# An FFN unit's first product is copied by ScalarE into the PSUM bank on which TensorE adds the second

## The chip, the core and the metric

The kernel runs on one core of a Trainium2 chip. The metric is the device time of one execution in microseconds (us). Before the change it is 1089.62 us, the median of three runs (1089.29 to 1091.97). Five engines work side by side, each through its own queue in order: TensorE (PE; its weight loads are PEld), VectorE (DVE), ScalarE (ACT), GpSimd (POOL) and SyncE (SP, which issues the loads). They wait for each other by semaphores.

## The reference

One layer of a backbone for 512 noisy tokens and 128 context tokens, 1024 features each: a gated recurrence, a spatial gating MLP and a pooling mixer, merged by gates, then a ConvFFN. The change touches the ConvFFN alone:

```python
def conv_ffn(x, w_up, conv_w, conv_b, w_down):
    h = x @ w_up                                  # 1024 -> 2 * 2816
    hp = jnp.pad(h, ((0, 0), (1, 1), (0, 0)))
    h = hp[:, :-2] * conv_w[0] + hp[:, 1:-1] * conv_w[1] + hp[:, 2:] * conv_w[2] + conv_b
    a, b = jnp.split(h, 2, axis=-1)
    return (jax.nn.silu(a) * b) @ w_down
```

## The kernel before

Everything is float32. TensorE takes operands of a reduced type, so each is split into a high and a low part, and a product of 128 features is three matmuls (`mm3`, L194 to L196: high·high, high·low, low·high). ScalarE writes the high part (`high`, L1159), VectorE the low one (`low`, L1164).

The FFN's up-projection goes by units `p` of 128 features of `a` and the 128 features of `b` that multiply them: 22 units (`NFF`). Unit 0 is computed plainly. Units 1 to 21 multiply 2x2 blocks (two halves of the 1024 input features, two halves of 320 tokens) with seven products in place of eight. A product is 4 blocks of 128 features, 12 matmuls of 320 columns, which TensorE adds up in a PSUM bank. In the order in which TensorE makes them in a unit, and with the name of the operand by which a row of the trace tells them:

1. m1 = `A10` on `b11`, into bank a
2. m2 = `A11` on `b21`, into bank b
3. n5 = `s` on `q1`, into bank c
4. `t` on `q2`, added to bank a
5. `A22` on `q4`, added to bank a of the unit before (`last`)
6. `u` on `b22`, added to bank c
7. `w` on `t3`, added to bank a

Between them the banks are read out, since later products are added to the same bank. `evacuate(p, 0, ...)` (ScalarE, L1212) copies m1 out of bank a into `ev`, before `t` is added there; `evacuate(p, 1, ...)` copies n5 out of bank c before `u`; `evacuate(p, 2, ...)` copies bank a after `t`, before `w`. The first half of `a`'s features, `u[:, 0, 0:H]` = m1 + m2, is an add on VectorE (L1222, 128x320), which reads bank b and `ev`. The other three quarters are two adds on VectorE and one copy on ScalarE (L1423).

The convolution of a finished unit follows one unit later: `conv_first` (ScalarE, L1233) makes the middle tap and the bias, `conv_rest` (VectorE, L1239, two instructions) the outer taps, then SiLU (ScalarE, L1391) and the product with the other half (`ffn_gate`, VectorE, L1245). The weight blocks' sums for the next unit are VectorE's: `sums` (L1143, L1144) and `sums2` (L1149, L1150). What is split for the next unit: `A1` = raw weights, `s` = sum, `tu` = sums, `wA` = raw sums; nine buffers (`WBUFS`) hold the parts.

The order on TensorE, ScalarE, VectorE and GpSimd is the order in which the code issues the instructions (`manual_schedule`); no planner is at work in this stage. Each waits at its place until the semaphores that it needs are there, and all behind it on its engine wait with it. From unit 3 on (`EARLY`) m1 and m2 of a unit are issued in its own turn of the loop; m1 and m2 of units 1 and 2 are made ahead of the loop. `u` has two buffers, `ev` two, PSUM eight banks.

After the 22 units TensorE makes the down-projection (L194 to L196 on `ah`).

Of the kernel before, what the change touches and what calls it, by code (L numbers as in the profile page):

```python
# [9 lines left out]
F32 = mybir.dt.float32  # L10
F32R = mybir.dt.float32r
I32 = mybir.dt.int32
AF = mybir.ActivationFunctionType
# [3 lines left out]
P = 128  # L17
# [8 lines left out]
H = HALF  # L26
# [37 lines left out]
def block_kernel(ctx: ExitStack, tc, x_prompt, x_sample, state, w_ada, w_in, w_bhg, w_bsg,  # L64
# [3 lines left out]
    nc = tc.nc  # L68
    ctx.enter_context(tc.manual_schedule(engines={mybir.EngineType.PE}))

    def pool(stack, name, bufs=1, space=None, side="left"):
        kw = {"side": side}
        if space is not None:
            kw = {"space": space}
        return stack.enter_context(tc.tile_pool(name=name, bufs=bufs, reuse_waits="tile", **kw))
# [33 lines left out]
    def par(name, i=0, n=1):  # L109
        a = PK[name][0] + i  # L110
        return pk[:, a:a + n]
# [34 lines left out]
    def half_of(t, n):  # L146
        return t[:, n * HK:(n + 1) * HK, :]
# [43 lines left out]
    def mm3(out, ws, xs, first, last, more=False):  # L191

        (wh, wl), (xh, xl) = ws, xs
        nc.tensor.matmul(out, lhsT=wh, rhs=xh, start=first, stop=False, skip_group_check=more)  # L194
        nc.tensor.matmul(out, lhsT=wh, rhs=xl, start=False, stop=False, skip_group_check=more)  # L195
        nc.tensor.matmul(out, lhsT=wl, rhs=xh, start=False, stop=last, skip_group_check=more)  # L196
# [619 lines left out]
    hz = pool(hzst, "hz", side="right")  # L816
# [218 lines left out]
    def quarter(pl, name):  # L1035
        return tuple(pl.tile([P, HK, H], F32R, tag="bf", name=name + part, bufs=6) for part in "hl")

    b11, b21, b22 = (quarter(bp, name) for name in ("b11", "b21", "b22"))
# [84 lines left out]
    def up_tile():  # L1123
        return ps_f.tile([P, 512], F32, tag="up", name="up")[:]
# [9 lines left out]
    raws, forms, banks, us, evs, accs = {}, {}, {}, {}, {}, {}  # L1134

    def up_raw(p, s):
        return wraw(unit_parts(cols_unit(ffn_up, (p + s * NFF) * P)), KD)
# [14 lines left out]
    def high(p, what, src, room=None):  # L1152

        room = room or wpair(src)
        if len(src.shape) == 3 and src.shape[1] == HK:
            hi, lo = room[0][:, 0:HK, :], room[0][:, HK:KD, :]
        else:
            hi, lo = room
        nc.scalar.activation(hi, src, AF.Copy)  # L1159
        forms[p, what] = (hi, lo, src)  # L1160

    def low(p, what):
        hi, lo, src = forms[p, what]
        nc.vector.tensor_tensor(lo, src, hi.bitcast(F32), op=ALU.subtract)  # L1164

    def one_form():
        return (wpool.tile([P, 1024], F32R, tag="w", name="ws", bufs=WBUFS)[:].rearrange("p (k c) -> p k c", k=KD),)

    def of(p, what, n=None):
        hi, lo = forms[p, what][0:2]  # L1170
        return (hi, lo) if n is None else (half_of(hi, n), half_of(lo, n))
# [18 lines left out]
    def product(p, what, bank, xs, first=False):  # L1190
        if what[0:2] == "A1":
            hi, lo = forms[p, "A1"][0:2]
            n = int(what[2])
            ws = (half_of(hi, n), lo[n] if isinstance(lo, list) else half_of(lo, n))
        elif what == "s":
            ws = of(p, "s")
        else:
            ws = of(p, *{"t": ("tu", 0), "u": ("tu", 1), "w": ("wA", 0), "A22": ("wA", 1)}[what])
        for k in range(HK):
            mm3(bank[:, 0:H], tuple(w[:, k, :] for w in ws), tuple(x[:, k, :] for x in xs),  # L1200
                first and k == 0, k == HK - 1, not first)

    def early(p, n):
        if n == 0:
            banks[p, "a"] = up_tile()
            product(p, "A10", banks[p, "a"], b11, True)
        else:
            banks[p, "b"] = up_tile()
            product(p, "A11", banks[p, "b"], b21, True)

    def evacuate(p, n, bank):
        nc.scalar.activation(evs[p][:, n, :], bank[:, 0:H], AF.Copy)  # L1212

    def pieces(u, half):

        if half == 0:
            return [(u[:, 0:H], slice(0, H))]
        return [(u[:, H:TS], slice(0, TS - H)), (u[:, TS + GAP:TF], slice(TS - H, H))]

    def add_to(u, half, bank, ev):  # L1220
        for to, c in pieces(u, half):
            nc.vector.tensor_tensor(to, bank[:, c], ev[:, c], op=ALU.add)  # L1222

    def conv_weight(p, s, r):

        return nconv[:, 3 * p + r:3 * p + r + 1] if s and p else par("conv_w", 3 * (p + s * NFF) + r)

    def conv_first(p, s, tag):

        jj = p + s * NFF  # L1230
        w = conv_weight(p, s, 1)
        accs[p, s] = hz.tile([P, TF], F32, tag=tag, name="acc", bufs=2)
        nc.scalar.activation(accs[p, s][:], us[p][:, s, :], AF.Identity, bias=par("conv_b", jj), scale=w)  # L1233

    def conv_rest(p, s):
        w0, w2 = (conv_weight(p, s, r) for r in (0, 2))
        acc, u = accs[p, s], us[p][:, s, :]
        for w, o, x in ((w0, acc[:, 1:TF], u[:, 0:TF - 1]), (w2, acc[:, 0:TF - 1], u[:, 1:TF])):
            nc.vector.scalar_tensor_tensor(o, x, w, o, op0=ALU.mult, op1=ALU.add)  # L1239

    def clear_gap(p, s):
        nc.gpsimd.memset(us[p][:, s, TS:TS + GAP], 0.0)
# [30 lines left out]
    EARLY = 3  # L1273
# [77 lines left out]
    for p in range(1, NFF + 1):  # L1351
        real, last, nxt = p < NFF, p - 1, p + 1 < NFF
        summed = last > 0
        if nxt:
            for s in range(2):
                if (p + 1, s) not in raws:
                    raws[p + 1, s] = up_raw(p + 1, s)

        if real and p >= EARLY:
            early(p, 0)  # L1360
        conv_first(last, 0, "gz")
        if summed:
            add_to(us[last][:, 1, :], 1, banks[last, "a"], evs[last][:, 1, :])
            clear_gap(last, 1)
        if real:
            low(p, "wA")

        if real:
            if p >= EARLY:
                early(p, 1)  # L1370
            evs[p] = hz.tile([P, 4, H], F32, tag="xk", name="ev", bufs=2)
            evacuate(p, 0, banks[p, "a"])
        conv_rest(last, 0)

        if real:
            banks[p, "c"] = up_tile()
            product(p, "s", banks[p, "c"], q1, True)
            if nxt and p + 1 >= EARLY:
                high(p + 1, "A1", raws[p + 1, 0])
            us[p] = hz.tile([P, 2, TF], F32, tag="tot", name="u", bufs=2)  # L1380
            add_to(us[p][:, 0, :], 0, banks[p, "b"], evs[p][:, 0, :])
            if nxt:
                sums(p + 1)

            product(p, "t", banks[p, "a"], q2)
            evacuate(p, 1, banks[p, "c"])
            if not summed:
                evacuate(p, 2, banks[p, "a"])
            if nxt:
                high(p + 1, "s", forms[p + 1, "sum"], one_form())  # L1390
        nc.scalar.activation(accs[last, 0][:], accs[last, 0][:], AF.Silu)  # L1391
        if nxt:
            if p + 1 >= EARLY:
                low(p + 1, "A1")
            low(p + 1, "s")

        if not real:
            pss = [[(slice(0, 512), up_tile())] for i in range(NT)]
            ws = unit(rows_unit(ffn_down, 0, 0), 0)
            for k in range(2):  # L1400
                for i in range(NT):
                    down(i, 0, k, ws)
        if summed:
            product(last, "A22", banks[last, "a"], q4)
        if real and summed:
            evacuate(p, 2, banks[p, "a"])
        if nxt:
            sums2(p + 1)
        elif real:
            fetch(1)  # L1410
            parts.update({(0, k): act_parts(k) for k in range(2)})
        else:
            fetch(1)
            parts.update({(0, k): act_parts(k) for k in range(2, 4)})

        if real:
            product(p, "u", banks[p, "c"], b22)
        if summed:
            ffn_gate(last - 1)
        if nxt:  # L1420
            high(p + 1, "tu", raws[p + 1, 0])
        if summed:
            nc.scalar.activation(us[last][:, 1, 0:H], banks[last, "a"][:, 0:H], AF.Copy)  # L1423
        if nxt:
            low(p + 1, "tu")

        if real:
            product(p, "w", banks[p, "a"], t3)
        conv_first(last, 1, "sig")
        if nxt:  # L1430
            high(p + 1, "wA", raws[p + 1, 1])
        if real:
            add_to(us[p][:, 0, :], 1, banks[p, "c"], evs[p][:, 2, :])
            clear_gap(p, 0)
        conv_rest(last, 1)
# [156 lines left out]
```

## Time and profile before

| | |
|---|---|
| median of three runs | 1089.62 us |
| the profiled execution, its own time | 1089.21 us |
| its span in the trace | 1087.4 us |
| outside the span | 1.8 us |
| units 1 to 21 of the FFN | about 666 to 935 us of the span |
| down-projection | about 926 to 1080 us |
| TensorE busy | 1059.7 us (97%) |
| VectorE busy | 761.2 us (70%) |
| ScalarE busy | 505.5 us (46%) |

A matmul's record is longer than the distance to the next one, since matmuls overlap in the array: rows of TensorE are read by the distance of their starts. The same holds in a smaller measure on VectorE and ScalarE, where the next instruction starts some hundredths of a microsecond before the record of the one ahead ends. A number in brackets behind a row is the idle time ahead of it and the engine that ended it. In the windows, PEclk is the clock that TensorE was granted, as a share of its full speed.

### The profile page before, as it was taken

Reading aid. Unit: us, or ns where it says so; the run is one execution under the profiler, and the core shown is the slowest. Engines: PE = TensorE matmul, PEld = TensorE weight load, DVE = VectorE, ACT = ScalarE, POOL = GpSimd, SP = SyncE. Lnnn points to the kernel's source line nnn. Section 1 sums busy time; section 2 is a strip of 40 time slices with the busy share of each in tenths; the row PEclk is TensorE's granted clock in tenths of the full one; section 3 lists DMA queues with packets and bytes.
Section 4 is the critical chain, followed back from the end, with each engine's and each line's share of the span. In section 5 each row is a group of like instructions: output and inputs, shape, how many; then the busy total and the mean of one; then the engine's idle time right before and its main releaser. Section 6 shows DMA issues by size and latency. Waiting matters only on the chain.

```text
span 1087.4 us, 17828 instructions
## 1 busy us (share of the span) xinstructions
PE 1059.7 (97%) x7258; PEld 989.7 (91%) x7258; DVE 761.2 (70%) x1141; ACT 505.5 (46%) x846; POOL 43.2 (4%) x111
## 2 busy tenths in 40 slices
PE   6999999999999999999999998999999999999997
PEld 4789999988999999999998888999999999888886
DVE  5586845677454767768365588999999998854634
ACT  5565533244324344533332356555555555643432
POOL 1030000000000000000000110000000000000201
PEclk9999999999999999999999999999999999999999
DMA  9964556535373121211135321322223222622202
GB/s 291 334 220 127 184 157 183 189 105 182 93 233 125 48 68 47 62 30 40 44 99 193 117 78 59 91 85 79 78 78 91 85 87 89 252 97 78 78 1 97
DMA packets 151618, 126.98 MB, mean 117 GB/s; under 512 B 4688, under 2 KB 131936, under 8 KB 151024
## 3 DMA queue, kind: packets, MB, share of 16 engines
q1 hardware_dynamic: 150816, 124.53, 36.9%
q8 instruction: 57, 0.93, 0.4%
q10 hardware_dynamic: 720, 1.31, 0.3%
q14 instruction: 25, 0.20, 0.1%
HBM read 115.32 MB, written 10.50 MB: 116 GB/s over the span
## 4 chain that ended last, share of the span: by engine, by line
PE 67%; DVE 24%; ACT 4%; issue 4%; DMA 2%; SPq 0%; POOL 0%; POOLq 0%; DVEq 0%; ACTq 0%
DVE wl L1164 7%; PE up L196 6%; PE up L195 6%; PE mm L195 6%; PE mm L194 6%; PE mm L196 6%; PE up L194 6%; DVE acc L1239 5%; PE q L194 4%; PE q L195 4%; PE q L196 4%; PE scores L891 4%; DVE u L1222 3%; ACT wh L1159 2%; PE px L194 2%
## 5 line engine op out<-in xcount | busy, mean ns | idle before, releaser
L125 DVE TENSOR_TENSOR wl<-raw,wh 128x1024 fp32r<-128x1024 f32 (+1 forms) x105 | 123.7, 1182 | 91.3 <-ACT wh L124 35.9
L124 ACT ACTIVATE wh<-raw 128x1024 fp32r<-128x1024 f32 (+1 forms) x105 | 107.2, 1022 | 63.1 <-PE q L195 28.6
L194 PE MATMUL mm<-h1h,wh 128*128 128x320 f32 x384 | 122.8, 320 | 0.0
L196 PE MATMUL mm<-h1h,wl 128*128 128x320 f32 x384 | 118.6, 309 | 0.0
L195 PE MATMUL mm<-h1l,wh 128*128 128x320 f32 x384 | 118.6, 309 | 0.0
L195 PE MATMUL up<-wl,ah 128*128 128x512 f32 (+1 forms) x242 | 89.9, 372 | 0.2 <-DVE wl L125 0.2
L196 PE MATMUL up<-wh,ah 128*128 128x512 f32 (+1 forms) x242 | 89.6, 370 | 0.1
L194 PE MATMUL up<-wh,ah 128*128 128x512 f32 (+1 forms) x242 | 89.7, 371 | 0.0
L1159 ACT ACTIVATE wh<-raw 128x1024 fp32r<-128x1024 f32 x63 | 66.2, 1051 | 43.1 <-DVE raw L1150 43.1
L1164 DVE TENSOR_TENSOR wl<-raw,wh 128x1024 fp32r<-128x1024 f32 x63 | 76.9, 1220 | 9.7 <-ACT wh L1159 9.6
L195 PEld LDWEIGHTS mm<-h1l,wh 128*128 128x128 f32 x384 | 72.3, 188 | 0.0
L194 PEld LDWEIGHTS mm<-h1h,wh 128*128 128x128 f32 x384 | 72.3, 188 | 0.0
L196 PEld LDWEIGHTS mm<-h1h,wl 128*128 128x128 f32 x384 | 72.1, 188 | 0.0
L124 ACT ACTIVATE ah<-act 128x512 fp32r<-128x512 f32 x88 | 36.2, 462 | 64.4 <-PE up L196 62.6
L125 DVE TENSOR_TENSOR ah<-act,ah 128x512 fp32r<-128x512 f32 x88 | 38.8, 486 | 33.0 <-ACT ah L124 33.0
L194 PE MATMUL q<-h1h,wh 128*128 128x320 f32 x192 | 60.0, 313 | 0.0
L196 PE MATMUL q<-h1h,wl 128*128 128x320 f32 x192 | 59.3, 309 | 0.0
L195 PE MATMUL q<-h1l,wh 128*128 128x320 f32 x192 | 59.3, 309 | 0.0
L195 PEld LDWEIGHTS up<-wl,ah 128*128 128x128 f32 x242 | 45.6, 188 | 8.7 <-DVE wl L125 0.9
L196 PEld LDWEIGHTS up<-wh,ah 128*128 128x128 f32 x242 | 45.6, 188 | 8.2 <-DVE ah L125 0.4
L194 PEld LDWEIGHTS up<-wh,ah 128*128 128x128 f32 x242 | 45.6, 188 | 7.9
L1159 ACT ACTIVATE ws<-s 128x512 fp32r<-128x512 f32 x21 | 13.3, 633 | 60.6 <-DVE s L1143 60.6
(373 smaller groups left out, 2996.0 us busy)
## 6 DMA issues: line engine op xcount, KB each, us to landing
raw<-in_w_in SPq DMA_DIRECT2D x56, 512.0 KB
raw<-in_ffn_up SPq DMA_DIRECT2D x44, 512.0 KB
raw<-in_w_ada SPq DMA_DIRECT2D x32, 512.0 KB
raw<-in_ffn_down SPq DMA_DIRECT2D x22, 512.0 KB
raw<-in_w_ada SPq DMA_DIRECT2D x32, 256.0 KB
raw<-in_w_out SPq DMA_DIRECT2D x8, 512.0 KB
x2scr<-x SPq DMA_DIRECT2D x5, 512.0 KB
x<-x2scr SPq DMA_DIRECT2D x1, 2560.0 KB
```

Source lines behind the costliest of these rows:

```text
L124: nc.scalar.activation(hi, src, AF.Copy)
L125: nc.vector.tensor_tensor(lo, src, hi.bitcast(F32), op=ALU.subtract)
L194: nc.tensor.matmul(out, lhsT=wh, rhs=xh, start=first, stop=False, skip_group_check=more)
L195: nc.tensor.matmul(out, lhsT=wh, rhs=xl, start=False, stop=False, skip_group_check=more)
L196: nc.tensor.matmul(out, lhsT=wl, rhs=xh, start=False, stop=last, skip_group_check=more)
L891: nc.tensor.matmul(px[:, i, :], lhsT=ck[:, i * P:(i + 1) * P], rhs=rhs(i), start=True, stop=True)
L1159: nc.scalar.activation(hi, src, AF.Copy)
L1164: nc.vector.tensor_tensor(lo, src, hi.bitcast(F32), op=ALU.subtract)
L1222: nc.vector.tensor_tensor(to, bank[:, c], ev[:, c], op=ALU.add)
L1239: nc.vector.scalar_tensor_tensor(o, x, w, o, op0=ALU.mult, op1=ALU.add)
```

## The change

For units 3 to 21 (`seeded`), ScalarE copies m1 from bank a into bank b, at the head of its work for the unit, and TensorE adds m2 there (`product` without `first`). n5 moves between m1 and m2 on TensorE. Bank b then holds m1 + m2; ScalarE copies it to `u[:, 0, 0:H]`, after n5's copy, and VectorE's add is gone. For units 1 and 2 the add stays, and m1's copy moves ahead of `conv_first`.

```diff
-        if real and p >= EARLY:
+        seeded = real and p >= EARLY
+        if seeded:
             early(p, 0)
+            banks[p, "b"] = up_tile()
+            nc.scalar.activation(banks[p, "b"][:, 0:H], banks[p, "a"][:, 0:H], AF.Copy)
+        elif real:
+            evs[p] = hz.tile([P, 4, H], F32, tag="xk", name="ev", bufs=2)
+            evacuate(p, 0, banks[p, "a"])
         conv_first(last, 0, "gz")
         if summed:
             add_to(us[last][:, 1, :], 1, banks[last, "a"], evs[last][:, 1, :])
             clear_gap(last, 1)
         if real:
             low(p, "wA")
-
-        if real:
-            if p >= EARLY:
-                early(p, 1)
-            evs[p] = hz.tile([P, 4, H], F32, tag="xk", name="ev", bufs=2)
-            evacuate(p, 0, banks[p, "a"])
         conv_rest(last, 0)
...
             us[p] = hz.tile([P, 2, TF], F32, tag="tot", name="u", bufs=2)
-            add_to(us[p][:, 0, :], 0, banks[p, "b"], evs[p][:, 0, :])
+            if seeded:
+                evs[p] = hz.tile([P, 4, H], F32, tag="xk", name="ev", bufs=2)
+
+                product(p, "A11", banks[p, "b"], b21)
+            else:
+                add_to(us[p][:, 0, :], 0, banks[p, "b"], evs[p][:, 0, :])
             if nxt:
                 sums(p + 1)

             product(p, "t", banks[p, "a"], q2)
             evacuate(p, 1, banks[p, "c"])
+            if seeded:
+                nc.scalar.activation(us[p][:, 0, 0:H], banks[p, "b"][:, 0:H], AF.Copy)
```

ScalarE, one unit in the middle of the FFN, before: from the copy of the unit before last to SiLU. `up_7481` is this unit's bank a, `up_7517` its bank c; L1212 is a copy into `ev`, L1233 `conv_first`, L1159 a high part.

```order
L1423 ACTIVATE u_7265<-up_7213 128x320
L1233 ACTIVATE acc_7467<-u_7265,pk_96,nconv_5886 128x644
L1159 ACTIVATE wh_7469<-raw_7345 128x1024
L1233 ACTIVATE acc_7494<-u_7399,pk_96 128x644
L1212 ACTIVATE ev_7513<-up_7481 128x320
L1159 ACTIVATE wh_7530<-raw_7477 128x1024
L1212 ACTIVATE ev_7513<-up_7517 128x320
L1159 ACTIVATE ws_7551<-s_7535 128x512
L1391 ACTIVATE acc_7494<-acc_7494 128x644
```

The same stretch on ScalarE in the changed kernel, where `up_7481` is bank a, `up_7494` bank b and `up_7504` bank c.

```order
L1430 ACTIVATE u_7252<-up_7213 128x320
L1233 ACTIVATE acc_7467<-u_7252,pk_96,nconv_5886 128x644
L1159 ACTIVATE wh_7469<-raw_7345 128x1024
L1363 ACTIVATE up_7494<-up_7481 128x320
L1233 ACTIVATE acc_7496<-u_7386,pk_96 128x644
L1159 ACTIVATE wh_7517<-raw_7477 128x1024
L1212 ACTIVATE ev_7521<-up_7504 128x320
L1393 ACTIVATE u_7520<-up_7494 128x320
L1159 ACTIVATE ws_7551<-s_7534 128x512
L1398 ACTIVATE acc_7496<-acc_7496 128x644
```

The copy of bank a (L1212 before, L1363 now) has moved ahead of `conv_first`, writes a bank instead of `ev`, and a copy of bank b (L1393) has come in ahead of `ws`.

TensorE, another unit, before: the end of m1 (`b11`) and what follows it.

```order
L194 MATMUL up_7347<-b11h_5877,wh_7262 128x320
L195 MATMUL up_7347<-b11l_5878,wh_7262 128x320
L196 MATMUL up_7347<-b11h_5877,wl_7263 128x320
L194 MATMUL up_7366<-b21h_5879,wh_7262 128x320
L195 MATMUL up_7366<-b21l_5880,wh_7262 128x320
L196 MATMUL up_7366<-b21h_5879,wl_7263 128x320
```

The same unit on TensorE in the changed kernel, at the start of m2 (`b21`).

```order
L194 MATMUL up_7370<-q1h_6384,ws_7283 128x320
L195 MATMUL up_7370<-q1l_6385,ws_7283 128x320
L196 MATMUL up_7370<-q1h_6384,ws_7283 128x320
L194 MATMUL up_7360<-b21h_5879,wh_7249 128x320
L195 MATMUL up_7360<-b21l_5880,wh_7249 128x320
L196 MATMUL up_7360<-b21h_5879,wl_7250 128x320
```

m2 stood right behind m1, and now stands behind n5 (`q1`), one product later.

## Rows read from the trace of the kernel before

**Rows 1.** The page: busy time of each engine, its share of the span, and its instructions.

```profile
PE 1059.7 (97%) x7258; PEld 989.7 (91%) x7258; DVE 761.2 (70%) x1141; ACT 505.5 (46%) x846; POOL 43.2 (4%) x111
```

**Rows 2.** The chain of waits in the stretch from 706 to 909 us: share of the stretch by engine and line.

```profile
by line: DVE wl L1164 28.2%; DVE acc L1239 20.0%; issue 11.9%; DVE u L1222 11.1%; ACT wh L1159 8.4%; DVE raw L1150 5.5%; DVE raw L1149 4.8%; DVE s L1143 4.8%; DVE ws L1164 4.7%; DVE raw L1144 0.3%; DVEq L1144 0.2%; ACTq L1159 0.1%
```

**Rows 3.** The windows, 693.1 to 909 us: length, busy us (and instructions) of PE, PEld, DVE, ACT and POOL, granted clock, DMA share, GB/s.

```profile
693.10:909.00 215.90, 213.85 (x1431) 209.54 (x1430) 205.92 (x307) 123.25 (x187) 2.25 (x34) 1.00 0.29 84
```

**Rows 4.** The timeline of VectorE over one unit: start us, us, engine, line, operation, out<-in.

```profile
756.74 0.48 DVE L1222 TENSOR_TENSOR u<-up,ev 128x320 f32<-128x320 f32 x1
757.14 0.68 DVE L1143 TENSOR_TENSOR s<-raw 128x512 f32<-128x512 f32 x1
...
760.92 0.69 DVE L1150 TENSOR_TENSOR raw<-raw 128x512 f32<-128x512 f32 x1
...
762.80 1.23 DVE L1164 TENSOR_TENSOR wl<-raw,wh 128x1024 fp32r<-128x1024 f32 x1 [0.45 <-ACT wh L1159]
...
767.73 1.81 DVE L1239 SCALAR_TENSOR_TENSOR acc<-u,pk,acc 128x643 f32<-128x643 f32 x2
769.45 0.48 DVE L1222 TENSOR_TENSOR u<-up,ev 128x320 f32<-128x320 f32 x1
769.85 0.69 DVE L1143 TENSOR_TENSOR s<-raw 128x512 f32<-128x512 f32 x1
```

**Rows 5.** The timeline of ScalarE over the same unit.

```profile
757.86 0.64 ACT L1159 ACTIVATE ws<-s 128x512 fp32r<-128x512 f32 x1 [3.11 <-DVE s L1143]
758.40 0.73 ACT L1391 ACTIVATE acc<-acc 128x644 f32<-128x644 f32 x1
759.03 0.41 ACT L1212 ACTIVATE ev<-up 128x320 f32<-128x320 f32 x1
761.71 1.06 ACT L1159 ACTIVATE wh<-raw 128x1024 fp32r<-128x1024 f32 x1 [2.27 <-DVE raw L1150]
762.68 0.42 ACT L1423 ACTIVATE u<-up 128x320 f32<-128x320 f32 x1
...
764.02 1.04 ACT L1159 ACTIVATE wh<-raw 128x1024 fp32r<-128x1024 f32 x1
764.97 0.91 ACT L1233 ACTIVATE acc<-u,pk 128x644 f32<-128x644 f32 x1
765.79 0.41 ACT L1212 ACTIVATE ev<-up 128x320 f32<-128x320 f32 x1
766.10 1.05 ACT L1159 ACTIVATE wh<-raw 128x1024 fp32r<-128x1024 f32 x1
767.05 0.42 ACT L1212 ACTIVATE ev<-up 128x320 f32<-128x320 f32 x1
770.57 0.63 ACT L1159 ACTIVATE ws<-s 128x512 fp32r<-128x512 f32 x1 [3.10 <-DVE s L1143]
```

**Rows 6.** The timeline of TensorE over the same unit: the end of `u`, the start of `w`, then the first matmul of m1, m2, n5 and `t`.

```profile
759.05 0.31 PE L196 MATMUL up<-b22h,wl 128*128 128x320 f32 x1
759.50 0.41 PE L194 MATMUL up<-t3h,wh 128*128 128x320 f32 x1
759.75 0.31 PE L195 MATMUL up<-t3l,wh 128*128 128x320 f32 x1
...
761.36 0.31 PE L194 MATMUL up<-b11h,wh 128*128 128x320 f32 x1
...
763.12 0.31 PE L194 MATMUL up<-b21h,wh 128*128 128x320 f32 x1
...
764.88 0.31 PE L194 MATMUL up<-q1h,ws 128*128 128x320 f32 x1
...
766.64 0.31 PE L194 MATMUL up<-q2h,wh 128*128 128x320 f32 x1
```

**Rows 7.** Two groups of ScalarE's instructions from 690 to 909 us (count, busy us, mean ns of one, idle us before them), and one short instruction from its timeline.

```profile
L1159 ACT ACTIVATE wh<-raw 128x1024 fp32r<-128x1024 f32 x52 | 54.6, 1051 | 38.5 <-DVE raw L1150 38.5
L1212 ACT ACTIVATE ev<-up 128x320 f32<-128x320 f32 x52 | 21.7, 416 | 0.0
...
944.29 0.29 ACT L124 ACTIVATE ah<-act 128x128 fp32r<-128x128 f32 x1
```

**Rows 8.** Units 2 and 3: TensorE's timeline around `t` of unit 2, a window of the stretch behind it (columns as in Rows 3), the first matmul of m2 of unit 3, and ScalarE's `conv_first` at the head of unit 3.

```profile
673.15 0.31 PE L196 MATMUL up<-q1h,ws 128*128 128x320 f32 x1
676.89 0.63 PE L194 MATMUL up<-q2h,wh 128*128 128x320 f32 x1 [3.43 <-ACT ev L1212]
...
678.00:679.00 1.00, 1.00 (x6) 1.00 (x5) 1.00 (x2) 0.11 (x1) 0.00 (x0) 0.50 0.11 32
...
687.13 0.31 PE L194 MATMUL up<-b21h,wh 128*128 128x320 f32 x1
...
688.69 0.91 ACT L1233 ACTIVATE acc<-u,pk 128x644 f32<-128x644 f32 x1
```

**Rows 9.** TensorE's timeline: the first and the last of 17 starts of `w` that stand 0.43 to 0.45 us behind the matmul ahead of them, and the first two matmuls of the down-projection's block behind unit 21.

```profile
708.64 0.42 PE L194 MATMUL up<-t3h,wh 128*128 128x320 f32 x1
...
912.02 0.42 PE L194 MATMUL up<-t3h,wh 128*128 128x320 f32 x1
...
934.80 0.48 PE L194 MATMUL up<-wh,ah 128*128 128x512 f32 x1
935.52 0.50 PE L195 MATMUL up<-wl,ah 128*128 128x512 f32 x1 [0.24 <-DVE wl L125]
```

## The prediction

> **What bounds the kernel now.** First the page: TensorE is busy 97% of the span, VectorE 70%, ScalarE 46% [rows 1]. A busy TensorE tells little by itself, so the chain of waits comes next, for the stage that is changed. From 706 to 909 us it names hardly any TensorE line: VectorE's low parts, convolution, adds and sums, then one of ScalarE's high parts [rows 2]. The line of the change, L1222, has 11.1% of it. The windows say the clock is at its upper level there (granted 1.00, 2.4 GHz) and the DMA engines are busy 0.29 [rows 3], so loads and clock are out of it.
>
> VectorE's timeline gives the pace: L1143 starts at 757.14 and again at 769.85, one unit in 12.71 us, with one stop of 0.45 us, for ScalarE's high part of `tu` [rows 4]. That part itself follows VectorE's L1150 by 0.79 us (760.92 to 761.71) [rows 4, 5]. VectorE's own work and this one hand-over are the loop.
>
> TensorE is close behind. From m1's first matmul (761.36) to `t`'s (766.64) are 36 matmuls in 5.28 us, 0.1467 each [rows 6]; a unit's 84 take 12.32 us. The missing 0.40 is seen at `w`: its first matmul stands 0.45 behind its forerunner and its second 0.25 behind the first, 0.30 and 0.10 beyond 0.147 [rows 6]. It waits for bank a's copy, which ScalarE ends at 759.44 [rows 5], three steps behind VectorE's L1143. So TensorE waits because VectorE is slow, and 0.39 us a unit is all that can be had before TensorE bounds.
>
> **VectorE's add goes.** L1222 on 320 columns starts at 769.45 and the next at 769.85 [rows 4]: 0.40 us in the queue. It goes in units 3 to 21, 19 times. In 21 VectorE goes from the convolution to a wait anyway, so I count 18: 7.2 us on VectorE's chain. Its loop becomes 12.71 - 0.40 = 12.31 us, TensorE's is 12.32. A tie; TensorE is late next.
>
> **ScalarE.** The copy that read m1 at 765.79 goes to 764.97, the end of the part written from 764.02, where `conv_first` stood [rows 5]. `conv_first` shifts by the distance 765.79 to 766.10, 0.31 us, and then ends near 766.2; VectorE's convolution takes it up at 767.73 [rows 4]. That cover of 1.5 us hides it. The high part at 766.10 and n5's copy at 767.05 keep their places. The new copy of bank b is 0.42 like its neighbours, behind n5's copy, in a hole: ScalarE is idle 3.10 us there until L1143's sum comes at 770.57 [rows 5], 0.40 sooner in future. The copy needs m2's end (below, about 767.4), ends near 767.9, and 2.2 us of the hole remain. Without that cover it would cost its 0.42. No DMA is moved and none is added; SyncE's loads stay where they are.
>
> **The copy into a bank is new.** No row shows ScalarE writing PSUM. From below it is bounded by its shortest neighbour, 0.29 us on 128 columns, from above by the 1.05 us that it takes over 1024 columns, and the nearest row is the copy of the same 320 columns out of the same bank into `ev`, 0.416 on 52 instances [rows 7]. I take 0.42. Within these ends the sum hardly moves, because of what the next part finds: at 0.29 it gains nothing, at 1.05 it delays the first seeded m2 by 0.63 us, once, and `conv_first` still ends 0.9 us ahead of its reader. The Trainium skill ("ScalarE: Activation LUTs", section "Step-by-step: what each stage is for") says that ScalarE is faster to PSUM than to SBUF; by it the copy is below 0.42 and the sum is the same, but no run so far shows it, and it bears on the chance of the slow copy below.
>
> **TensorE's new wait.** m2 now waits for this copy, and behind it on TensorE stand `t`, `A22`, `u`, `w` and the next m1. In VectorE's frame the copy ends at 764.97 + 0.42 = 765.39; the hand-over from ScalarE takes 0.06 (759.44 to 759.50 [rows 5, 6]), so m2 may start at 765.45, plus the 0.10 that a start after a wait costs. TensorE would be there with n5 done at 764.88 if it went on as before. But once pushed to 765.55 it stays there: four products (m2, `t`, `A22`, `u`) of 1.76 us bring `w` to 772.59, whose bank copy ends at 759.44 + 12.71 - 0.40 = 771.75, so the old wait is gone with 0.8 us to spare; three more (`w`, m1, n5) bring the next m2 to 777.87, and its copy is ready at 765.45 + 12.31 = 777.76. No wait again. The new wait is paid once, and then TensorE runs through, 0.1 us behind the copy.
>
> How much once? m2 of unit 3 starts at 687.13 [rows 8]. Now n5 is made there, 1.76 us to 688.89. The copy stands at the head of ScalarE's unit, 688.69 [rows 8], ends at 689.11, and m2 starts at 689.17 + 0.10. So `t` starts at 691.0 instead of 687.13 + 3.52 = 690.65: 0.4 us later than before, with an idle TensorE of 0.3 us ahead of m2, or more, since in unit 2 m1's copy comes one `conv_first` (0.9 us) sooner and shortens the 3.43 us that `t` waits there [rows 8]. That gain is swallowed at m2 of unit 3. Behind the 3.43 us the clock was at its lower level (granted 0.50, 1.2 GHz, in 678 to 679 [rows 8]); I count neither gain nor loss for it.
>
> **The sum.** 17 starts of `w` wait, 708.64 to 912.02 [rows 9], 0.40 each: 6.8 us go, 0.4 come. TensorE ends unit 21's stretch with the matmul at 934.80 and is free at 934.95; that becomes 934.95 - 6.8 + 0.4 = 928.55. There it had waited until 935.52 for VectorE's low part [rows 9]; VectorE comes 7.2 sooner, at 928.3, and does not hold it. 935.52 - 928.55 = 7.0 us. Behind it TensorE bounds to the end and just shifts. The profiled execution's 1089.21 (span 1087.4 and 1.8 around it) becomes 1082.2; it lies 0.4 below the median of the runs shown, so I forecast 1082.6.
>
> **Rivals.**
>
> *Waits that change places (1084.5 to 1086.3).* The two loops tie at 12.31 and 12.32, and every stop costs TensorE 0.10 beyond the wait. If it stops at m2 or `w` in each unit, 0.10 to half of the 0.40 stays: 18 units of 0.1 to 0.2 are 1.8 to 3.6 us of the 7.0. For it speaks that nothing has slack; against it that TensorE, once late, is not waited for (0.8 us at `w`) and that VectorE's only stop is not on TensorE.
>
> *No gain (1089).* The 0.40 comes back whole, because the copy, queued behind three long ScalarE instructions, holds each m2. For that the copy would have to slip by 0.4 more every unit; all that stands ahead of it is released by VectorE alone [rows 4, 5], and only a longer ScalarE chain could do it.
>
> *Slower: a slow copy (1096 or more).* The path m1's end, copy, m2, `t`, `A22`, `u`, `w`, m1 closes on itself: six products, 10.56 us, plus 0.16 from a matmul's last start to its end beyond the usual distance, 0.06 twice for the hand-overs, 0.10 for the restart, and the copy: 10.94 + copy. n5 alone (1.76) lies beside it. At 0.42 it is 11.4, with 0.9 us of slack. It decides above 1.38 us, eats the gain at 1.77, and at twice the longest row, 2.1 us [rows 7], a unit takes 13.04: 18 x 0.33 = 6 us slower, and the start's loss. Against it stands every ScalarE row: the 52 copies of 320 columns take 0.416 in the mean [rows 7]. The skill's sentence on ScalarE and PSUM, named above, would rule it out, if it holds here.
>
> **How the numbers follow.** Forecast 0.70 (its own range 1081.2 to 1084, for the 0.05 us by which a loop of 18 units may be misread either way, 0.9 us, and the 1.0 us gained in unit 2 should TensorE keep it), waits that change places 0.14, no gain 0.07, slower 0.09. A measurement of this kernel tells 0.3%, 3.3 us, from no change; the first two are faster than that, so faster 0.84, same 0.07, slower 0.09. The range takes the forecast and nearly all of the first rival: 1080.9 to 1086.6.
>
> **What would show it.** Right: L1143 to L1143 in 12.3 us; no idle time ahead of `t3h`; the copy into the bank near 0.42; no wait of `b21h` behind unit 3 or 4; the copy of bank b inside ScalarE's hole, which shrinks to about 2.2; the chain of waits in the FFN going over to TensorE. Wrong: a stop at `b21h` in each unit (first rival; with a copy above 1.4 us, the last), a period above 12.5 us, VectorE's stop ahead of `tu`'s low part grown beyond 0.45, or a gain that is lost again at 930 us.

## The result, and the profile after

The changed kernel takes 1081.37 us (median of 6 runs, 1080.69 to 1082.40) against 1089.45 us for the kernel before (6 runs, 1088.87 to 1091.97): a ratio of 0.9921, 95% interval 0.9908 to 0.9934. The profiled execution took 1081.27 us, with a span of 1079.5, against 1089.21 and 1087.4. The forecast was 1082.6, in a range of 1080.9 to 1086.6.

The page first, busy time by engine, which answers to [rows 1]:

```profile
PE 1053.2 (98%) x7258; PEld 987.6 (91%) x7258; DVE 753.5 (70%) x1122; ACT 514.3 (48%) x865; POOL 42.8 (4%) x111
```

VectorE has 19 instructions fewer and 7.7 us less work, ScalarE 19 copies more and 8.8 us more work; TensorE has the same 7258 matmuls. Busy time has moved from VectorE to ScalarE, which is no gain by itself. What the kernel gained stands in the chain of waits, from 706 to 900 us (share of the stretch by engine and line):

```profile
by line: PE up L195 33.4%; PE up L196 33.4%; PE up L194 33.2%
```

In [rows 2] VectorE's lines had about four fifths of the stretch and TensorE's none. Now TensorE's three lines have all of it, and nothing stands between them. The windows say the same (length, then busy us and instructions of PE, PEld, DVE, ACT and POOL, granted clock, DMA share, GB/s):

```profile
693.10:905.00 211.90, 211.90 (x1447) 211.90 (x1446) 201.87 (x293) 132.81 (x207) 2.24 (x34) 1.00 0.30 87
```

TensorE is busy for 211.90 of 211.90 us; in [rows 3] it was busy for 213.85 of 215.90, at the same granted clock of 1.00.

One unit on VectorE, whose lines answer to [rows 4] (start us, us, engine, line, operation, out<-in, and in brackets the idle time before it and its releaser):

```profile
754.41 0.69 DVE L1143 TENSOR_TENSOR s<-raw 128x512 f32<-128x512 f32 x1
...
758.20 0.69 DVE L1150 TENSOR_TENSOR raw<-raw 128x512 f32<-128x512 f32 x1
...
760.08 1.23 DVE L1164 TENSOR_TENSOR wl<-raw,wh 128x1024 fp32r<-128x1024 f32 x1 [0.45 <-ACT wh L1159]
...
765.01 1.81 DVE L1239 SCALAR_TENSOR_TENSOR acc<-u,pk,acc 128x643 f32<-128x643 f32 x2
766.73 0.69 DVE L1143 TENSOR_TENSOR s<-raw 128x512 f32<-128x512 f32 x1
```

L1143 to L1143 is 12.32 us (754.41 to 766.73) instead of 12.71: the next sum follows the convolution directly, and the stop ahead of `tu`'s low part is the same 0.45. ScalarE in the same unit, which answers to [rows 5]:

```profile
755.13 0.63 ACT L1159 ACTIVATE ws<-s 128x512 fp32r<-128x512 f32 x1 [2.15 <-DVE s L1143]
...
762.25 0.42 ACT L1363 ACTIVATE up<-up 128x320 f32<-128x320 f32 x1
762.60 0.91 ACT L1233 ACTIVATE acc<-u,pk 128x644 f32<-128x644 f32 x1
763.42 1.04 ACT L1159 ACTIVATE wh<-raw 128x1024 fp32r<-128x1024 f32 x1
764.36 0.41 ACT L1212 ACTIVATE ev<-up 128x320 f32<-128x320 f32 x1
764.87 0.44 ACT L1393 ACTIVATE u<-up 128x320 f32<-128x320 f32 x1
767.45 0.63 ACT L1159 ACTIVATE ws<-s 128x512 fp32r<-128x512 f32 x1 [2.14 <-DVE s L1143]
```

L1363 is the copy from bank a into bank b: 0.42 us here. L1393, the copy of bank b, takes 0.44 and lies in ScalarE's hole, which has shrunk from 3.10 to 2.14 us. By groups, from 690 to 900 us (count, busy us, mean ns of one, idle us before them), against [rows 7]:

```profile
L1212 ACT ACTIVATE ev<-up 128x320 f32<-128x320 f32 x35 | 14.5, 415 | 0.0
...
L1363 ACT ACTIVATE up<-up 128x320 f32<-128x320 f32 x17 | 7.1, 417 | 0.0
```

A copy of 320 columns costs ScalarE the same here whether it writes a tile (415 ns) or a bank (417 ns).

TensorE, first in unit 3 (n5's last matmul, m2's first), and then the same places as in [rows 6] and [rows 9]:

```profile
688.12 0.31 PE L196 MATMUL up<-q1h,ws 128*128 128x320 f32 x1
688.84 0.42 PE L194 MATMUL up<-b21h,wh 128*128 128x320 f32 x1 [0.40 <-ACT up L1363]
...
757.43 0.31 PE L196 MATMUL up<-b22h,wl 128*128 128x320 f32 x1
757.58 0.31 PE L194 MATMUL up<-t3h,wh 128*128 128x320 f32 x1
...
762.86 0.31 PE L194 MATMUL up<-b21h,wh 128*128 128x320 f32 x1
...
928.08 0.39 PE L194 MATMUL up<-wh,ah 128*128 128x512 f32 x1
928.31 0.40 PE L195 MATMUL up<-wl,ah 128*128 128x512 f32 x1
928.54 0.40 PE L196 MATMUL up<-wh,ah 128*128 128x512 f32 x1
928.78 0.40 PE L194 MATMUL up<-wh,ah 128*128 128x512 f32 x1
```

The new wait, 0.40 us for L1363, stands once, at m2 of unit 3. `w` (`t3h`) follows its forerunner by 0.15 us where it was 0.45, and behind unit 21 the down-projection's block starts without a stop. In the trace of the kernel before, the second of these stood late, as [rows 9] show. The next two stood late as well, and so did the last two of three matmuls some 6 us on (TensorE of the kernel before, then two low parts on VectorE at the same places):

```profile
936.12 0.50 PE L196 MATMUL up<-wh,ah 128*128 128x512 f32 x1
936.46 0.40 PE L194 MATMUL up<-wh,ah 128*128 128x512 f32 x1
...
942.60 0.39 PE L194 MATMUL up<-wh,ah 128*128 128x512 f32 x1
942.96 0.50 PE L195 MATMUL up<-wl,ah 128*128 128x512 f32 x1
943.29 0.40 PE L196 MATMUL up<-wh,ah 128*128 128x512 f32 x1
```

```profile
935.38 0.68 DVE L125 TENSOR_TENSOR ah<-act,ah 128x512 fp32r<-128x512 f32 x1
...
941.68 1.22 DVE L125 TENSOR_TENSOR wl<-raw,wh 128x1024 fp32r<-128x1024 f32 x1
```

These places come back below.

**How the executions are compared.** The FFN doesn't begin at the same time in every execution. A mark that both kernels share ahead of the changed units is the low part of q4, on VectorE, here in the kernel before and then in the changed one:

```profile
664.62 1.49 DVE L125 TENSOR_TENSOR q4l<-h,q4h 128x1280 fp32r<-128x1280 f32 x1 [1.34 <-ACT q4h L124]
```

```profile
664.30 1.49 DVE L125 TENSOR_TENSOR q4l<-h,q4h 128x1280 fp32r<-128x1280 f32 x1 [1.34 <-ACT q4h L124]
```

Nothing that the change touches runs ahead of it, and yet it starts anywhere from 664.2 to 667.8 in the profiles of this study. So beside the times I compare the stretch from this start to the end of the span: before 1087.4 - 664.62 = 422.8 us, after 1079.5 - 664.30 = 415.2.

### The profile page after: what moved, and what is told of

The parts are those of the page before. It is cut to its first block, busy times and chain, and to the rows that moved or that the text cites. A ratio compares the mean times of both kernels' runs of the same rounds, so it can differ in the third digit from the quotient of the medians.

```text
span 1079.5 us, 17822 instructions
## 1 busy us (share of the span) xinstructions
PE 1053.2 (98%) x7258; PEld 987.6 (91%) x7258; DVE 753.5 (70%) x1122; ACT 514.3 (48%) x865; POOL 42.8 (4%) x111
## 4 chain that ended last, share of the span: by engine, by line
PE 90%; DVE 5%; ACT 1%; DMA 1%; issue 1%; SPq 0%; POOL 0%; POOLq 0%; DVEq 0%; ACTq 0%
PE up L196 14%; PE up L195 13%; PE up L194 13%; PE mm L194 6%; PE mm L195 6%; PE mm L196 6%; PE q L194 4%; PE q L195 4%; PE q L196 4%; PE scores L891 4%; PE px L194 2%; PE px L196 2%; PE px L195 2%; PE ada L278 1%; PE zi L194 1%
## 5 line engine op out<-in xcount | busy, mean ns | idle before, releaser
L1159 ACT ACTIVATE wh<-raw 128x1024 fp32r<-128x1024 f32 x63 | 66.1, 1049 | 43.1 <-DVE raw L1150 43.0
L904 ACT ACTIVATE ck<-xk 128x640 f32<-128x640 f32 x28 | 22.3, 795 | 40.1 <-PE scores L891 34.7
```

Of the source, the lines that this page charges most:

```text
L904: nc.scalar.activation(ck[:].rearrange("p (b s m) -> p b s m", s=2, m=m), level_view(xk, 0, T, m), AF.Copy)
```

## The experiments

The cuts of code are against the changed kernel unless the text says that they are against the kernel before. Theory A is the prediction's: VectorE's add was the 0.40 us by which its loop was longer than TensorE's, and with it gone TensorE runs through. The rivals of A change from run to run and stand with each.

**Only the order.** Does the gain come from the places (n5 between m1 and m2, the copies at the head of ScalarE's unit), not from the add? The add stays, on VectorE; m2 gets a bank of its own and nothing is written into it by ScalarE.

```diff
         if seeded:
             early(p, 0)
-            banks[p, "b"] = up_tile()
-            nc.scalar.activation(banks[p, "b"][:, 0:H], banks[p, "a"][:, 0:H], AF.Copy)
-        elif real:
+        if real:
             evs[p] = hz.tile([P, 4, H], F32, tag="xk", name="ev", bufs=2)
             evacuate(p, 0, banks[p, "a"])
...
-                evs[p] = hz.tile([P, 4, H], F32, tag="xk", name="ev", bufs=2)
-
-                product(p, "A11", banks[p, "b"], b21)
-            else:
-                add_to(us[p][:, 0, :], 0, banks[p, "b"], evs[p][:, 0, :])
+                early(p, 1)
+            add_to(us[p][:, 0, :], 0, banks[p, "b"], evs[p][:, 0, :])
...
-            if seeded:
-                nc.scalar.activation(us[p][:, 0, 0:H], banks[p, "b"][:, 0:H], AF.Copy)
```

> Both moves of the change without the copy into the bank: m1's copy at the head of ScalarE's unit but into ev, n5 between m1 and m2 on TensorE, VectorE's add on 320 columns kept. Theory A (the gain is VectorE's add, 0.40 us in a loop of 12.71): a unit takes 12.71 us again, TensorE waits at w again, and the time is that of the kernel before, 1089.5 us, within 1. Theory B (the gain is the order: m1's copy sooner, or n5 in the gap): a unit takes about 12.3 us and the time is about 1081.5.

It measured 1089.25 us beside 1089.25 for the kernel before: ratio 1.000 [0.9991, 1.0009]. The chain (706 to 900 us) is VectorE's again, with the add in it:

```profile
by line: DVE wl L1164 27.6%; DVE acc L1239 19.7%; DVE u L1222 11.2%; ACT wh L1159 8.3%; issue 7.3%; DVE raw L1144 5.7%; DVE raw L1150 5.4%; DVE raw L1149 5.1%; DVE s L1143 5.0%; DVE ws L1164 5.0%; ACTq L1159 0.1%
```

The unit is back at 12.71 us (L1143 at 756.84 and 769.55), and `w` stands 0.42 to 0.50 us behind its forerunner again in units 3 to 20 (0.42 to 0.45 in the kernel before, in units 4 to 20). Theory B falls: the order is worth nothing by itself, it only makes room for the sum in the bank.

**Only the add.** The other half: the kernel before, in its own order, with the add of units 3 to 21 left out (the sum of m1 and m2 is not made; ScalarE copies m2 alone). The cut is against the kernel before.

```diff
-            add_to(us[p][:, 0, :], 0, banks[p, "b"], evs[p][:, 0, :])
+            if p < EARLY:
+                add_to(us[p][:, 0, :], 0, banks[p, "b"], evs[p][:, 0, :])
...
             evacuate(p, 1, banks[p, "c"])
+            if p >= EARLY:
+                nc.scalar.activation(us[p][:, 0, 0:H], banks[p, "b"][:, 0:H], AF.Copy)
```

> The kernel before in its old order, but in units 3 to 21 the sum of m1 and m2 is left out: VectorE's add is gone and ScalarE copies m2 alone into u, behind n5's copy, as the changed kernel does with the sum. There is no copy into a bank, no new wait of m2 and no new order on TensorE. Theory A: a unit takes 12.31 to 12.33 us and the time is 1080.8 to 1082, that of the changed kernel or up to 0.5 us less. Theory B: 1089 us.

1081.98 us, ratio 0.993 [0.9914, 0.9947], and a chain (706 to 900 us) that is TensorE's alone:

```profile
by line: PE up L195 33.5%; PE up L196 33.4%; PE up L194 33.2%
```

The stretch from q4's low part is 415.4 us, 0.2 from the changed kernel's. A holds: the whole gain is the add's.

**Is VectorE's queue what counts, or this add?** If it is the queue, 0.86 us less of something else on VectorE does the same to the kernel before, and nothing more to the changed one. One of the two outer taps of half b's convolution is left out from unit 2 on, in both.

```diff
-        for w, o, x in ((w0, acc[:, 1:TF], u[:, 0:TF - 1]), (w2, acc[:, 0:TF - 1], u[:, 1:TF])):
+        taps = ((w0, acc[:, 1:TF], u[:, 0:TF - 1]), (w2, acc[:, 0:TF - 1], u[:, 1:TF]))
+        for w, o, x in taps if s == 0 or p < 2 else taps[0:1]:
```

In the changed kernel:

> The changed kernel, where VectorE leaves out one of the two outer taps of b's half of the convolution from unit 2 on, one instruction of 0.86 us a unit. Theory A (TensorE bounds the units now, 84 matmuls of 0.1467 us): the time stays within 1 us of 1081.4, a unit takes 12.31 us. Theory C (VectorE's loop of 12.31 us still sets the pace and TensorE only happens to be as long): a unit takes about 11.5 us and the time falls by up to 15 us.

In the kernel before:

> The kernel before, where VectorE leaves out the same outer tap of b's half, 0.86 us a unit, and nothing else is changed. Theory A: VectorE's loop falls to 11.85 us, but TensorE lets only 0.39 of the 0.86 us through: a unit takes 12.32 us and the time is 1081 to 1082. Theory C (the pace is VectorE's alone): 18 x 0.86 = 15 us less, about 1074. Theory B (the order): 1089.

The changed kernel without the tap takes 1081.69 us, 0.9932 [0.9917, 0.9946] of before: no faster than with it. VectorE's timeline shows where its 0.86 us went:

```profile
752.57 1.81 DVE L1240 SCALAR_TENSOR_TENSOR acc<-u,pk,acc 128x643 f32<-128x643 f32 x2 [0.84 <-ACT acc L1233]
...
764.89 1.81 DVE L1240 SCALAR_TENSOR_TENSOR acc<-u,pk,acc 128x643 f32<-128x643 f32 x2 [0.84 <-ACT acc L1233]
```

VectorE spends them on a wait, 0.84 us in each unit, and the unit stays at 12.32 (752.57 to 764.89). The kernel before without the tap takes 1081.85 us, 0.9931 [0.9916, 0.9946]: the add is still there, and the gain is as large as the changed kernel's. The window shows that TensorE has no gap left:

```profile
693.10:905.00 211.90, 211.90 (x1447) 211.90 (x1446) 199.17 (x298) 130.58 (x191) 2.26 (x34) 1.00 0.30 88
```

Of 0.86 us only 0.39 passes into the unit. So TensorE's 12.32 us is the floor, and 0.39 us taken from VectorE at either of two places reaches it: A again, while B (the order) and C (VectorE still bounds) fall.

**How much may the copy into the bank cost?** It is made three and five times over (the last writes the same values).

```diff
-            nc.scalar.activation(banks[p, "b"][:, 0:H], banks[p, "a"][:, 0:H], AF.Copy)
+            for _ in range(3):
+                nc.scalar.activation(banks[p, "b"][:, 0:H], banks[p, "a"][:, 0:H], AF.Copy)
```

> The changed kernel with the copy of m1 into the bank made three times, one behind the other (the same values each time). Each repeat waits for the one ahead, so the three take about 1.3 us. Theory A (the closed path m1, copies, m2, t, A22, u, w, m1 is 10.94 us plus the copies, and free up to 12.32): 12.26 us, still hidden; only m2 of unit 3 comes 0.9 us later, and the time is 1081.8 to 1083. Theory D (the copy lies on the path of each unit): 18 x 0.9 us more, about 1097.

> The changed kernel with the copy of m1 into the bank made five times, about 2.2 us. Theory A: the closed path is 10.94 + 2.2 = 13.1 us a unit, TensorE stops at m2 in each unit for about 0.8 us, and the time is 18 x 0.8 + 1.8 us more, 1095 to 1100. Theory E (what a long copy delays is conv_first and by it VectorE's convolution, 764.97 + 2.1 + 0.92 against 767.70): 0.3 us a unit, about 1088, with VectorE idle ahead of the convolution and no stop at m2 beyond that.

Three copies in a row take 1.33 us, and the kernel 1082.75 us, 0.9942 [0.9924, 0.996]. The wait stands at m2 of unit 3 alone, and has grown by 0.91:

```profile
693.25 0.42 PE L194 MATMUL up<-b21h,wh 128*128 128x320 f32 x1 [1.31 <-ACT up L1364]
```

The stretch from q4's low part is 0.9 us longer than the changed kernel's (416.1 against 415.2): the copy is paid once. Five copies take 2.23 us, and the kernel 1098.18 us, 1.0087 [1.0071, 1.0103]: slower than before. Now every m2 stops:

```profile
756.28 0.42 PE L194 MATMUL up<-b21h,wh 128*128 128x320 f32 x1 [0.56 <-ACT up L1364]
...
769.43 0.42 PE L194 MATMUL up<-b21h,wh 128*128 128x320 f32 x1 [0.56 <-ACT up L1364]
```

A unit takes 13.15 us, and E, which put this kernel at 1088 us, falls. The closed path of the prediction, 10.94 + copy, gives 10.94 + 2.23 = 13.17 here and 12.27 at three copies, just below TensorE's 12.32. That is the edge from both sides: a copy of 1.33 us is hidden, one of 2.23 is not.

**Units 1 and 2.** There the change moves m1's copy ahead of `conv_first` too. Here it stands where it stood.

```diff
-        elif real:
-            evs[p] = hz.tile([P, 4, H], F32, tag="xk", name="ev", bufs=2)
-            evacuate(p, 0, banks[p, "a"])
...
             low(p, "wA")
+        if real and not seeded:
+            evs[p] = hz.tile([P, 4, H], F32, tag="xk", name="ev", bufs=2)
+            evacuate(p, 0, banks[p, "a"])
```

> The changed kernel, but in units 1 and 2 m1's copy into ev stands behind conv_first as before. Theory A: TensorE's wait at t of unit 2 is 3.4 us again, perhaps with the clock at its lower level behind it as before, but all of it is swallowed at m2 of unit 3, which waits for ScalarE; the time stays within 0.7 us of 1081.4. Theory F (what the changed kernel gained beyond the forecast is the clock's dip at unit 2 that is gone): 1 to 2.5 us more, 1082.5 to 1084.

1081.88 us, 0.9937 [0.9922, 0.9953]; the stretch is 415.1 us, as in the changed kernel. TensorE's timeline shows both ends of it:

```profile
676.76 0.64 PE L194 MATMUL up<-q2h,wh 128*128 128x320 f32 x1 [3.43 <-ACT ev L1212]
...
689.02 0.41 PE L194 MATMUL up<-b21h,wh 128*128 128x320 f32 x1
```

The 3.43 us and the lower clock behind it are there again (matmuls 0.267 us apart from 676.76 to 679.86), and m2 of unit 3 starts as late, 24.54 us behind q4's low part, because the copy sets it. What is gained in unit 2 is swallowed there, and F falls.

**Can the stop in unit 2 be had as well?** Unit 2 is made as the later ones are, m1 into the bank and m2 behind n5.

```diff
-    early(2, 1)
...
-        seeded = real and p >= EARLY
+        seeded = real and p >= 2
         if seeded:
-            early(p, 0)
+            if p >= EARLY:
+                early(p, 0)
```

> The changed kernel with unit 2 treated like units 3 to 21: its m2 is no longer made ahead of the loop but on top of the copied m1, and its add on VectorE is gone. Theory A: VectorE is the bound up to unit 3, so its chain is 0.40 us shorter and m2 of unit 3 starts 0.4 us sooner: 1081.0 against 1081.4. TensorE's product falls into its idle time at unit 2. Rival: m2 of unit 2 in the loop makes TensorE late at unit 3, and the time rises by up to 1 us.

1082.86 us, 0.9952 [0.9934, 0.997], the rival's side. The output is wrong in this run: m1's part is taken to be missing from unit 2's sum (see the next one). TensorE's timeline, and the window behind its stop:

```profile
676.54 0.41 PE L194 MATMUL up<-b21h,wh 128*128 128x320 f32 x1 [2.77 <-ACT up L1363]
...
690.49 0.31 PE L194 MATMUL up<-b21h,wh 128*128 128x320 f32 x1
```

```profile
677.00:678.00 1.00, 1.00 (x5) 1.00 (x4) 1.00 (x2) 1.00 (x2) 0.03 (x1) 0.50 0.86 246
```

Behind the stop of 2.77 us the granted clock is 0.50 (1.2 GHz), to about 680. m2 of unit 3 comes 690.49 - 665.25 = 25.24 us behind q4's low part, against 24.54 in the changed kernel. VectorE did come 0.40 us sooner, as A has it (L1143 of unit 3 at 15.84 us behind q4's low part, against 16.24); but no wait stands ahead of m2, so here TensorE itself is late.

Theory G for the missing part: TensorE adds to what ScalarE wrote only on columns that a matmul had written last. By the order in which the code asks for banks, unit 2's bank had last held transposes of 128 columns, where units 3 to 21 get banks that held 320-column products. So, on top of the last edit, one matmul of 320 columns goes into the bank ahead of ScalarE's copy.

```diff
+    banks[2, "b"] = up_tile()
+    nc.tensor.matmul(banks[2, "b"][:, 0:H], lhsT=half_of(forms[2, "A1"][0], 1)[:, 0, :], rhs=b21[0][:, 0, :],
+                     start=True, stop=True)
```

> The kernel with unit 2 treated like units 3 to 21, and one matmul of 320 columns written into unit 2's bank b ahead of the loop; ScalarE's copy of m1 then overwrites what it wrote. Without that matmul the last writers of that bank are 128-column transposes, and m1 did not arrive in unit 2's sum. Theory G (TensorE adds to what ScalarE wrote only in columns that its own last writes to the bank had covered): m1 is in the sum now. Theory H (the copy of unit 2 comes too early or too late for another reason): it is still missing. Time: that of the kernel without the matmul, 1081.5 to 1083.

The output is right now, so m1 is in unit 2's sum. It took 1082.54 us, 0.9937 [0.9922, 0.9952]:

```profile
677.02 0.41 PE L194 MATMUL up<-b21h,wh 128*128 128x320 f32 x1 [2.77 <-ACT up L1367]
...
689.86 0.41 PE L194 MATMUL up<-b21h,wh 128*128 128x320 f32 x1 [0.26 <-ACT up L1367]
```

The same stop of 2.77 us, and the clock stayed up this time. m2 of unit 3 comes 689.86 - 665.72 = 24.14 us behind q4's low part, 0.40 sooner than in the changed kernel, as A has it. The stretch is 415.0 us, 0.2 shorter, and the times can't tell that.

**Relief for VectorE at the start.** GpSimd, idle there, makes the second raw sum of units 2 and 3.

```diff
-        nc.vector.tensor_tensor(a21, a21, half_of(raws[p, 0], 0), op=ALU.add)
+        eng = nc.gpsimd if p in (2, 3) else nc.vector
+        eng.tensor_tensor(a21, a21, half_of(raws[p, 0], 0), op=ALU.add)
```

> The changed kernel, where GpSimd makes the second of the two sums of raw weights (128x512) for units 2 and 3, which nobody needs before the end of the unit. Theory A (up to m2 of unit 3 VectorE is the bound, behind it TensorE): VectorE's chain loses 0.61 us twice, m2 of unit 3 starts 1.2 us sooner, the time is 1080.2. Rival: GpSimd's add slows VectorE while it runs, or is too late for ScalarE's high part at the end of the unit; then 1081.4 or more.

1082.39 us, 0.9937 [0.9924, 0.9949]; the stretch is 416.3 us, 1.1 longer than in the changed kernel. GpSimd and VectorE:

```profile
670.97 1.30 POOL L1145 TENSOR_TENSOR raw<-raw 128x512 f32<-128x512 f32 x1 [26.09 <-DVE s L1143]
683.13 2.15 POOL L1145 TENSOR_TENSOR raw<-raw 128x512 f32<-128x512 f32 x1 [10.79 <-DVE s L1143]
...
671.54 1.28 DVE L1165 TENSOR_TENSOR ws<-s,ws 128x512 fp32r<-128x512 f32 x1 [0.70 <-ACT ws L1160]
682.91 1.22 DVE L1165 TENSOR_TENSOR wl<-raw,wh 128x1024 fp32r<-128x1024 f32 x1
684.05 1.78 DVE L1165 TENSOR_TENSOR ws<-s,ws 128x512 fp32r<-128x512 f32 x1
```

The first add saved VectorE nothing: in its place VectorE waits 0.70 us for ScalarE's high part of `s`, a wait that the add had filled. Only the second was work on VectorE's chain, so A's 0.61 us twice was wrong. Each time the low part of `s` that ran beside GpSimd's add took longer, 1.28 and 1.78 us where 0.69 is usual. From q4's low part to L1143 of unit 3 it is 16.82 us, against 16.24 in the changed kernel, and to m2 of unit 3 25.50, against 24.54. The rival was right.

None of the versions beats the changed kernel.

## Why the mechanism of the prediction was right, and which step failed

**Right.** The add was the 0.40 us. The unit became 12.32 us where 12.31 and 12.32 were worked out, every wait ahead of `w` went from unit 3 on, and the chain went over to TensorE. The two halves alone show why: the order without the add's removal gains nothing (1.000), the removal without the order gains all (0.993), and a tap in its place does as well (0.9931).

**Right: the copies.** 417 ns into the bank where 0.42 was taken; bank b's copy in a hole that shrank to 2.14 where 2.2 was left; VectorE's stop ahead of `tu` unchanged at 0.45.

**Right: the new wait once.** m2 of unit 3 was put at 689.17 in before's frame; it started at 688.84, in an execution whose FFN began 0.32 us earlier, which is 689.16. No later m2 waited. The gain of unit 2 was swallowed, as argued, but not all of it at m2 of unit 3: `t` of unit 2 came 0.98 us sooner, and `w` of unit 2, at 682.89, then stopped for 1.69 us, where it had not stopped before, and came only 0.40 sooner. Putting the copies of units 1 and 2 back left the stretch at 415.1.

**The step that failed: the hand-over behind unit 21.** The last term of the sum, 935.52 - 928.55 = 7.0 us, with "behind it TensorE bounds to the end and just shifts", was too small: the stretch from q4's low part became 7.6 us shorter. TensorE's arrival was right: its first matmul of the block behind unit 21 moved from 934.80 to 928.08, 6.72 us, of which 0.32 lies ahead of the FFN, so 6.40, which is the 6.8 - 0.4 of the prediction. What was mis-sized are the stops behind it, 1.2 us where the prediction counted 0.57 (935.52 - 934.95), a single one. The usual distance of these matmuls of 512 columns is 0.23 us, not the 0.15 of the units, so the second matmul stood 0.72 - 0.23 = 0.49 late. Four more stood late behind it: 935.52 to 936.12 is 0.60, 936.12 to 936.46 is 0.34, 942.60 to 942.96 is 0.36, and 942.96 to 943.29 is 0.34. That is 0.37 + 0.11 + 0.13 + 0.11 = 0.72 us which the prediction put at nothing. They have no bracket in the trace, since the matmul ahead is counted as busy for most of the time.

These were waits on VectorE too. The low parts in the rows above end at 936.06 and 942.90, and the matmuls of 936.12 and 942.96 start 0.06 us behind them, as long as the hand-over from ScalarE that the prediction took from its rows; the matmul behind each of these starts follows it by 0.34, 0.11 more than usual, like the second matmul of `w` in [rows 6]. In the changed kernel VectorE's low parts came 7.4 us sooner by the same count (the one of 935.38 at 927.64) and TensorE 6.4, so VectorE was ahead by 1.0 us more, and the four matmuls start 0.23 or 0.24 apart from 928.08 to 928.78. From the down-projection's first matmul (926.22 before, 919.50 after) to the end of the span it was 161.2 us and became 160.0. With the order alone it is 160.9, with the add left out 160.3, and with the tap left out of the kernel before 160.0; no run changes these stops one by one.

The rest of the 7.9 us between the two profiled executions is the 0.32 ahead of the FFN, which no part of the change touches. It is chance, and so is part of the distance of the forecast, 1082.6, from 1081.37: about 0.6 is the failed step, 0.3 the earlier start, and 0.3 is the median: the prediction put 0.4 on top of the profiled execution for it, and the changed kernel's median lies only 0.1 above its own.

**The rivals.** *Waits that change places* did not come at 0.42 us: TensorE, once 0.4 late, met no second wait. *No gain* needed a longer chain on ScalarE, and there is none. *A slow copy* was a true mechanism with the wrong price: five copies in a row turn it on, at the period its formula gives (13.15 for 13.17), and one copy of 0.417 us is far from it. The Trainium skill ("ScalarE: Activation LUTs", section "Step-by-step: what each stage is for") would have ruled it out with its sentence that ScalarE writes PSUM faster than SBUF. The runs rule it out otherwise: 417 ns against 415 is no faster for this copy.

## What to carry to other kernels

When two engines' loops are within a few tenths of a microsecond, work out both from the rows (start to start) before you price an edit: what the slower loop can gain ends where the other stands, here at 0.39 of an add's 0.40 or of a tap's 0.86. A sum of two products can be left to the bank if the copy into it has a product's time to hide behind, its closed path (products, hand-overs, copy) stays below the loop, and TensorE itself was the last to write the same columns of the bank; one wait at the start is then all that it costs. Where a stretch that gets faster hands over to another stage, count every late matmul behind the hand-over by its distance from the one ahead, with the usual distance of that stage, not only the one with a wait beside it.

## What was not expected of the hardware

**The clock behind the same stop.** TensorE stops for 2.77 us in unit 2 in the changed kernel and in several of the experiments. Behind it the granted clock fell to 0.50 in the run with unit 2 made as the others (0.267 us between matmuls up to 680.13), and it fell with five copies and with GpSimd's sum; it stayed at 1.00 in the changed kernel (its window follows), with the order alone, without the tap, with three copies and with the bank written first.

```profile
678.00:679.00 1.00, 1.00 (x9) 1.00 (x9) 1.00 (x2) 0.00 (x0) 0.00 (x0) 1.00 0.00 1
```

Nothing found in the traces tells the two groups apart, and it need not be the kernel: in six executions of the changed kernel the mean granted clock was 0.994 to 0.999, and 0.999 in the profiled one, which has no such fall, while the traces with the fall have 0.996 or 0.997. The times don't follow it (1080.69 us at 0.994, 1081.27 at 0.999). What decides it stays open. Behind the longer stop of 3.42 to 3.43 us the clock fell in all four traces that have one. With unit 2 made as the others, m2 of unit 3 came 25.24 us behind q4's low part with the lower clock and 24.14 without it; with units 1 and 2 put back the lower clock cost nothing, since the copy set that start.

**What a matmul adds to.** With unit 2's bank last written by 128-column transposes, the output was wrong; with one matmul of 320 columns into it first, it was right. That it was m1 that went missing is inferred from this pair; no run shows the bank itself. The Trainium skill ("PSUM — Partial Sum Buffer", section "The four PSUM rules") says that only TensorE changes the marks by which a matmul adds, that a matmul adds to what another engine wrote where the mark is set and overwrites it where it is clear, and that 0 is therefore the only seed that is safe in both cases. The two runs agree, and units 3 to 21 are the case in which another seed is kept: the bank's columns were TensorE's own before.

**VectorE beside GpSimd.** The same VectorE instruction took 0.69 us alone and 1.28 and 1.78 us beside GpSimd's add. The Trainium skill ("SBUF — State Buffer", section "Who interferes with whom") says that a VectorE instruction with two inputs in SBUF contends with a GpSimd instruction that reads SBUF; these rows agree. It is not always VectorE that pays: the low part at 682.91, also with two inputs, kept its 1.22 us beside about 1.0 us of GpSimd's second add, and that add took 2.15 us where the first took 1.30.
